# Half-row modulation units on TensorE beside the input products of the feed-forward blocks, and a later split of Strassen weight sums

## The chip, the cores and the metric

One NeuronCore of a Trainium2 chip runs the whole kernel in one launch; the other cores have nothing to do. The metric is device time in microseconds (us) from start to end of the program. The engines are named as in the profile: PE (TensorE; PEld is its weight load, which runs beside it), DVE (VectorE), ACT (ScalarE), POOL (GpSimd) and SP (SyncE, whose queue SPq issues nearly all DMAs here).

## The reference

Two layers; each is a feed-forward block (FFN), a mixer (retention and grouped attention in layer 0, neighbourhood attention in layer 1), and a second FFN, on 512 latent and 128 context tokens of width 1024. Each of the six sub-layers s takes three vectors (shift, scale, gate) from a modulation, a product of a conditioning vector with a 1024 x 9216 matrix per layer; latent and context tokens have a conditioning vector each.

```python
def swiglu(h, w_in, w_out):
    gate, up = jnp.split(h @ w_in, 2, axis=-1)
    return (jax.nn.silu(gate) * up) @ w_out            # D_FF = 2816

def adaln_sublayer(x, mod, s, g_pre, g_post, fn, weight):
    shift, scale, gate = mod[:, 3 * s, None], mod[:, 3 * s + 1, None], mod[:, 3 * s + 2, None]
    h = rmsnorm(x, g_pre) * (1 + scale) + shift
    y, aux = fn(h)
    return x + weight * gate * rmsnorm(y, g_post), aux

mod = (jax.nn.silu(cond) @ mod_w[l] + mod_b[l]).reshape(cond.shape[0], 9, 1024)
```

Everything is float32. A row of the modulation in what follows is one of the nine 1024-wide vectors of a layer, (layer, row); a half row is 512 columns of it, for both conditioning vectors.

## The kernel before

**Blocks and parts.** The four FFNs are called F1 to F4 in the order they run: layer 0 first and second, layer 1 first and second. Function `ffn` (L575 on) cuts the 22 column tiles of D_FF into six parts p0 to p5 of 2, 4, 4, 4, 4, 4 tiles (`PARTS`). A part has an input stage (activations times `w_in`, then SiLU and product, into tiles `g`) and an output stage (`g` times `w_out`, added into `yacc`). Parts p1 to p5 compute the input stage by Strassen's scheme: a `Unit` (L631) is one column tile, with seven products of twelve 128x320 matmuls (`product`, L645; one matmul is L647). `strassen` (L712) runs the products of four units interleaved, 28 places in all; after each place come `stream.pump()` and `tick()`. The place called fill runs the first output products. Then `products` (L741) runs the rest of the 120 output matmuls of 128x512 (L736), with a pump and a tick between groups.

Float32 precision comes from splitting each operand in a high and a low half and adding three products of halves. `split` (L349, L350) does so for activations: ACT copies (`g`, `b` tiles), DVE subtracts. In a unit ACT copies the intermediate sum out of PSUM (L677) before the next product may add to it, and DVE adds, multiplies and splits (L671 to L703).

**Weights.** `Stream` (L60) loads raw weights by DMAs on SP (L96) into three buffers, splits them on ACT (L156, `whi`) and DVE (L157, `wlo`) into five buffers, and for each unit has POOL form sums and differences of quarters (`_combine`, L142). One of these sums, S (the tile is called `G` or `macc` in the profile), is split by ACT and DVE too. The condition is in `_room`: the split of S comes no sooner than `PARTS_LAG` = 2 pumps after POOL's instructions were issued. An engine runs its queue in order, so what is queued behind the split on ACT waits with it.

**The modulation.** The start computes the first rows on PE (L894, with `cc32`, the conditioning vectors in columns 0 and 1 of a 32-column tile). The other 16 rows, 32 half rows, are made by the generator `mod_gen` (L359) during F1 (14 half rows), F2 (6) and F3 (12); F4 has none. A half row takes eight loads of 128 x 512 (256 KB, L369, two buffers), and per load two DVE operations, one for each conditioning vector: a TENSOR_SCALAR first (L382), then SCALAR_TENSOR_TENSOR (L384) into `macc`. The sum over the 128 partitions is four matmuls with ones (L406: two column halves for two conditioning vectors, each into its own 32-column group of PE), a DVE add of the bias (L410; bias loads at L396), and four small DMAs to DRAM (L415). `tick` asks the generator for steps at a rate that weighs a place of the output stage three times as much as one of the input stage (`OUT_SHARE` = 3).

**What sets the order.** The program is written place by place as above; a scheduler then sets the order of instructions within each engine's queue, so what is written behind a place can stand some instructions earlier or later. Buffers of a pool tag are reused in turn: a load waits until the buffer's last readers are done, and holds up SP's queue meanwhile.

## Time and profile before

| | us |
|---|---|
| time, median of 3 runs (lowest, highest) | 2821.89 (2818.86, 2822.24) |
| the profiled execution | 2815.01 |
| its span in the trace | 2813.1 |
| PE busy | 2557.8 (91%) |
| PE weight loads | 2257.3 (80%) |
| DVE busy | 2051.6 (73%) |
| ACT busy | 1176.1 (42%) |
| POOL busy | 723.6 (26%) |
| DMA, mean | 106 GB/s |
| chain that ended last: PE, DVE, DMA, POOL, issue, ACT | 33, 15, 6, 5, 4, 4% |

Shares of busy time are means over all stages of the program. PE's busy time counts matmuls with their pipeline, so that a gap between matmuls shows only where nothing is in flight. What a change in one stage is worth is read from that stage: the table of stretches gives the busy time of every engine between two times (one per group of parts in what follows), the timeline gives single pieces with the idle time before them in brackets and what ended it, and the list of waits adds such idle times up over the span. The lines that follow are of the code of before, numbered as in the listing above.

### The profile page before, as it was taken

The page shows a single profiled execution, that of the slowest core. Times are in us where ns is not written, and L with a number is a line of the kernel's source. Part 1 is how long each engine was busy: PE and PEld are TensorE (multiplying, and loading weights), DVE is VectorE, ACT ScalarE, POOL GpSimd, SP SyncE. Part 2 cuts the span into 40 slices and gives each one's busy share as a digit, 9 for nine tenths or more (in the row PEclk, how much of TensorE's full clock was granted, in tenths as well). Part 3 has the DMA queues.
Part 4 walks back from the last instruction along what each step waited for, and adds up shares of the span by engine and source line. Part 5 has one row for each costly group of instructions (what it writes and reads, how often), then busy time and mean ns, then how long its engine had stood idle before and what let it go on. Part 6 is the DMA issues. An engine that isn't in the chain of part 4 may idle for free.

```text
span 2813.1 us, 39476 instructions
## 1 busy us (share of the span) xinstructions
PE 2557.8 (91%) x15090; PEld 2257.3 (80%) x15090; DVE 2051.6 (73%) x3079; ACT 1176.1 (42%) x2179; POOL 723.6 (26%) x612
## 2 busy tenths in 40 slices
PE   7889876999999989999988998999899999999998
PEld 5778766888876788888877887788889978888887
DVE  5988886775577597787568988896777766655556
ACT  4423322364356443333354332233565555433333
POOL 1312322220001132323233222222532312323222
PEclk9999988999999999999999999999999999999999
DMA  8354564331110333343343444454222232222233
GB/s 237 105 150 133 153 174 125 106 117 55 56 49 16 94 116 108 107 129 82 98 135 116 130 145 119 130 151 123 86 67 65 65 100 75 83 80 62 77 105 112
DMA packets 358620, 297.85 MB, mean 106 GB/s; under 512 B 46352, under 2 KB 290976, under 8 KB 358432
## 3 DMA queue, kind: packets, MB, share of 16 engines
q1 hardware_dynamic: 353968, 282.24, 34.4%
q10 hardware_dynamic: 2880, 9.18, 0.8%
q0 software_dynamic: 1584, 3.93, 0.5%
q8 instruction: 118, 1.93, 0.3%
q14 instruction: 70, 0.57, 0.1%
HBM read 283.22 MB, written 15.97 MB: 106 GB/s over the span
## 4 chain that ended last, share of the span: by engine, by line
PE 33%; DVE 15%; DMA 6%; POOL 5%; issue 4%; ACT 4%; SPq 0%; DVEq 0%; ACTq 0%; POOLq 0%
PE ps L647 12%; PE ps L736 10%; DVE wlo L157 5%; PE ps L560 5%; DVE macc L384 4%; DMA mraw<-in_mod_w_dram 3%; POOL raw L142 2%; ACT whi L156 2%; PE ps L978 2%; POOL G L142 1%; DMA raw<-in_ffn_w_in_dram 1%; PE ps L550 1%; DMA raw<-in_ffn_w_out_dram 1%; DVE g L350 1%; PE ps L1925 1%
## 5 line engine op out<-in xcount | busy, mean ns | idle before, releaser
L156 ACT CAST whi<-raw 128x1024 fp32r<-128x1024 f32 x400 | 418.6, 1050 | 503.4 <-PE ps L736 239.4
L736 PE MATMUL ps<-whi,g 128*128 128x512 f32 x1760 | 586.6, 408 | 39.5 <-DVE g L350 19.8
L647 PE MATMUL ps<-hT,whi 128*128 128x320 f32 x2560 | 576.2, 313 | 2.0 <-DVE xn L688 1.9
L157 DVE TENSOR_TENSOR wlo<-raw,whi 128x1024 fp32r<-128x1024 f32 x400 | 500.1, 1253 | 103.8 <-ACT whi L156 95.7
L647 PE MATMUL ps<-b,whi 128*128 128x320 f32 x1920 | 448.2, 320 | 112.3 <-ACT xn L677 56.7
L142 POOL TENSOR_TENSOR raw<-raw 128x512 f32<-128x512 f32 x160 | 223.4, 1396 | 1256.9 <-DVE wlo L157 1191.1
L384 DVE SCALAR_TENSOR_TENSOR macc<-mraw,cc,macc 128x512 f32<-128x512 f32 x448 | 402.7, 931 | 71.7 <-DMA mraw<-in_mod_w_dram 70.9
L736 PEld LDWEIGHTS ps<-whi,g 128*128 128x128 f32 x1760 | 341.7, 195 | 135.0 <-DVE g L350 25.4
L647 PEld LDWEIGHTS ps<-hT,whi 128*128 128x128 f32 x2560 | 436.9, 192 | 8.0 <-DVE xn L688 2.6
L647 PEld LDWEIGHTS ps<-b,whi 128*128 128x128 f32 x1920 | 330.1, 194 | 134.7 <-ACT xn L677 65.7
L647 PE MATMUL ps<-hT,wlo 128*128 128x320 f32 x1280 | 399.6, 312 | 0.0
L736 PE MATMUL ps<-wlo,g 128*128 128x512 f32 x880 | 355.9, 404 | 0.0
L647 PE MATMUL ps<-b,wlo 128*128 128x320 f32 x960 | 303.6, 316 | 22.4 <-DVE wlo L157 22.4
L560 PE MATMUL ps<-hT,whi 128*128 128x384 f32 (+1 forms) x1216 | 277.6, 316 | 0.1
L647 PEld LDWEIGHTS ps<-hT,wlo 128*128 128x128 f32 x1280 | 244.6, 191 | 0.4 <-issue 0.4
L560 PEld LDWEIGHTS ps<-hT,whi 128*128 128x128 f32 x1216 | 203.9, 188 | 21.9 <-issue 15.2
L647 PEld LDWEIGHTS ps<-b,wlo 128*128 128x128 f32 x960 | 186.8, 195 | 22.8 <-DVE wlo L157 22.8
L736 PEld LDWEIGHTS ps<-wlo,g 128*128 128x128 f32 x880 | 171.7, 195 | 37.7 <-issue 0.4
L560 PE MATMUL ps<-hT,wlo 128*128 128x384 f32 (+1 forms) x608 | 188.6, 310 | 0.0
L156 ACT CAST whi<-G 128x512 fp32r<-128x512 f32 x72 | 44.6, 620 | 254.1 <-POOL G L142 118.7
L550 PE MATMUL ps<-hT,whi 128*128 128x384 f32 (+1 forms) x640 | 140.9, 311 | 4.8 <-DVE hT L350 4.8
L157 DVE TENSOR_TENSOR wlo<-G,whi 128x512 fp32r<-128x512 f32 x72 | 84.4, 1173 | 71.8 <-ACT whi L156 71.1
(402 smaller groups left out, 3846.2 us busy)
## 6 DMA issues: line engine op xcount, KB each, us to landing
raw<-in_ffn_w_in_dram SPq DMA_DIRECT2D x172, 512.0 KB
mraw<-in_mod_w_dram SPq DMA_DIRECT2D x256, 256.0 KB
raw<-in_ffn_w_out_dram SPq DMA_DIRECT2D x88, 512.0 KB
raw<-in_na_w_qkv_dram SPq DMA_DIRECT2D x24, 512.0 KB
raw<-in_ab_w_in_dram SPq DMA_DIRECT2D x22, 512.0 KB
raw<-in_mod_w_dram SPq DMA_DIRECT2D x32, 256.0 KB
xs<-x ACTq DMA_DIRECT2D x15, 512.0 KB
b<-xs SPq DMA_DIRECT2D x15, 512.0 KB
```

The source lines that it names most:

```text
L142: self.nc.gpsimd.tensor_tensor(out=out, in0=in0, in1=in1, op=op)
L156: self.nc.scalar.copy(hi[:, :k * n], raw[:, :k * n])
L157: self.nc.vector.tensor_tensor(out=lo[:, :k * n], in0=raw[:, :k * n], in1=hi[:, :k * n].bitcast(F32), op=ALU.subtract)
L350: return a, nc.vector.tensor_tensor(out=lo, in0=src, in1=hi.bitcast(F32), op=ALU.subtract)
L384: nc.vector.scalar_tensor_tensor(out=acc[c], in0=raw, scalar=w, in1=acc[c], op0=ALU.mult, op1=ALU.add)
L550: nc.tensor.matmul(out=banks[grp], lhsT=w[a][:, k, :], rhs=hT[b][:, k, o:o + n], start=(k == 0 and (a, b) == (0, 0)), stop=(k == NK - 1 an ...
L560: nc.tensor.matmul(out=banks[grp], lhsT=w[a][:, k, :], rhs=hT[b][:, k, o:o + n], start=(k == 0 and (a, b) == (0, 0)), stop=(k == NK - 1 an ...
L647: nc.tensor.matmul(out=out, lhsT=w[a][:, k, :], rhs=b[c][:, k, :], start=start and (k, a, c) == (0, 0, 0), stop=(k == 3 and (a, c) == PASS ...
L736: nc.tensor.matmul(out=out, lhsT=g[a][kf][:, t * 128:(t + 1) * 128], rhs=w[b], start=(kf == 0 and (a, b) == (0, 0)), stop=(kf == len(fts) ...
L978: nc.tensor.matmul(out=y[t][h], lhsT=hT[a][:, k, t * 128:(t + 1) * 128], rhs=ws[k // 2, h][b][:, k % 2, :], start=(k == 0 and (a, b) == (0 ...
L1925: nc.tensor.matmul(out=acc[r, c], lhsT=v, rhs=PT[hh][:, slot, c], start=(slot == 0), stop=(slot == 3))
```

## The change

The list `MOD_ROWS` deals the 16 rows to the blocks anew: F1 12 half rows (before 14), F2 8 (6), F3 10 (12), F4 2 (0). A class `Modulation` takes the place of `mod_gen`. It has units of two kinds. A "v" unit is the old way on DVE: one is written beside the output stage of each of p0 to p4 (in F4 of p0 and p1), 17 in all; its sum by ones falls to the next part's start. A "t" unit is on PE: the 32-column conditioning tile `cc32` is the stationary operand and the raw weights, 128 columns to each of four column groups of PE, the moving one; it has two steps of sixteen 32x128 matmuls (four row blocks of 128 times four column groups), each on two loads. They are written beside the input stage: two units in each of p1 to p3 and one in p4 of F1, one in p1 to p3 of F2, two in p1 and one in p2 to p4 of F3, none in F4: 15 in all. Loads are now of two row blocks (512 KB) in three buffers, a tag (`mod`) that the accumulator, the sums S of the last part and a scratch tile share; bias and result rows have one buffer (`mrow`) for two before. `PARTS_LAG` goes from 2 to 4: the split of S may come two pumps later. No tick follows the first `glu` calls of F1 any more.

```diff
-PARTS_LAG = 2
+PARTS_LAG = 4
...
+MOD_ROWS = {
+    (0, 0): [(0, 2), (0, 3), (0, 4), (0, 5), (0, 6), (0, 7)], (0, 2): [(0, 8), (1, 0), (1, 1), (1, 2)],
+    (1, 0): [(1, 3), (1, 4), (1, 5), (1, 6), (1, 7)], (1, 2): [(1, 8)],
+}
...
-OUT_SHARE = 3
...
-    def mod_gen(pool, todo):
...
+    class Modulation:
+        N = 512
+        STEPS = {"v": NK + 3, "t": 4}
+        def __init__(self, pool, todo):
+            self.pool = pool
+            self.units = [(l, r, h) for l, r in todo for h in range(D // self.N)]
+            self.loads = [(*u, q) for u in self.units for q in range(NK // 2)]
+            self.raws = []
+            self.cc32 = pool.tile([128, NK, 32], F32, tag="cc32", name="cc32", bufs=1)
+            nc.vector.memset(self.cc32, 0.0)
+            nc.vector.tensor_copy(self.cc32[:, :, 0:2], cc)
+            self.it, self.rate, self.owed = iter(()), 0.0, 0.0
+            self.load()
+        def load(self):
+            while self.loads and len(self.raws) < 2:
+                l, r, h, q = self.loads.pop(0)
+                raw = self.pool.tile([128, 2, self.N], F32, tag="mod", name="mod", bufs=3)
+                c0 = r * D + h * self.N
+                nc.sync.dma_start(out=raw, in_=kblock(I["mod_w"][l], 2 * q, 2, c0, self.N))
+                self.raws.append(raw)
+        def bias(self, l, c0, parts):
+            n = self.N // 2 if len(parts) == 4 and parts[0][1] == parts[2][1] else self.N // 4
+            row = self.pool.tile([128, 256], F32, tag="mrow", name="mrow", bufs=1)[:, 0:n]
+            for p, o in parts:
+                nc.sync.dma_start(
+                    out=row[p:p + 32, :], in_=I["mod_b"][l, c0 + o:c0 + o + n].partition_broadcast(32)
+                )
+            return row, n
+        def on_v(self, l, r, h):
+            c0 = r * D + h * self.N
+            parts = [(64 * c + 32 * e, 256 * e) for c in range(2) for e in range(2)]
+            row, n = self.bias(l, c0, parts)
+            acc = self.pool.tile([128, 2, self.N], F32, tag="mod", name="mod", bufs=3)
+            for k in range(NK):
+                raw = self.raws[0]
+                for c in range(2):
+                    w = cc[:, k, c:c + 1]
+                    if k == 0:
+                        nc.vector.tensor_scalar(out=acc[:, c], in0=raw[:, 0], scalar1=w, scalar2=None, op0=ALU.mult)
+                    else:
+                        nc.vector.scalar_tensor_tensor(
+                            out=acc[:, c], in0=raw[:, k % 2], scalar=w, in1=acc[:, c], op0=ALU.mult, op1=ALU.add
+                        )
+                if k % 2:
+                    self.raws.pop(0)
+                    if k < NK - 1:
+                        self.load()
+                yield
+            yield
+            yield
+            ps = bank([128, n])
+            for p, o in parts:
+                nc.tensor.matmul(
+                    out=ps[p:p + 32, :], lhsT=ones[:, 0:32], rhs=acc[:, p // 64, o:o + n], start=True, stop=True
+                )
+            nc.vector.tensor_tensor(out=row, in0=ps, in1=row, op=ALU.add)
+            for p, o in parts:
+                nc.sync.dma_start(out=modrows[l][r][p // 64:p // 64 + 1, h * self.N + o:h * self.N + o + n], in_=row[p:p + 1, :])
+            self.load()
+            yield
+        def on_t(self, l, r, h):
+            c0 = r * D + h * self.N
+            parts = [(32 * e, 128 * e) for e in range(4)]
+            row, n = self.bias(l, c0, parts)
+            ps = bank([128, n])
+            for q in range(NK // 4):
+                for i in range(2):
+                    raw = self.raws.pop(0)
+                    for k2 in range(2):
+                        k = 4 * q + 2 * i + k2
+                        for p, o in parts:
+                            nc.tensor.matmul(
+                                out=ps[p:p + 32, :], lhsT=self.cc32[:, k, :], rhs=raw[:, k2, o:o + n],
+                                start=(k == 0), stop=(k == NK - 1),
+                            )
+                self.load()
+                yield
+            nc.vector.tensor_tensor(out=row, in0=ps, in1=row, op=ALU.add)
+            for p, o in parts:
+                nc.sync.dma_start(out=modrows[l][r][:, h * self.N + o:h * self.N + o + n], in_=row[p:p + 2, :])
+            yield
+        def stage(self, kind, n, places):
+            for _ in self.it:
+                pass
+            us, self.units = self.units[:n], self.units[n:]
+            self.it = itertools.chain(*((self.on_v if kind == "v" else self.on_t)(*u) for u in us))
+            self.rate, self.owed = self.STEPS[kind] * len(us) / places, 0.0
+        def tick(self):
+            self.owed += self.rate
+            while self.owed >= 1.0:
+                self.owed -= 1.0
+                next(self.it, None)
...
-        side, steps = side or (iter(()), 0)
-        weight = sum(7 * n for n in PARTS[1:-1]) + sum(4 * n for n in PARTS[:-1]) * OUT_SHARE
-        rate, owed = steps / (weight - 6.0), 0.0
+        mod = Modulation(fp, todo)
+        n_v = len(PARTS) - 1
+        n_t = [0] + [max(len(mod.units) - n_v + 3 - p, 0) // 4 for p in range(4)]
...
-        def tick(share=1):
...
+        def tick():
             if prep:
                 prep.pop(0)()
+            mod.tick()
...
             else:
-                for _ in side:
-                    pass
-                stream.part_tile = lambda: fp.tile([128, 512], F32, tag="macc", name="macc", bufs=2)
+                mod.stage("t", len(mod.units), 1)
+                mod.stage("t", 0, 1)
+                stream.part_tile = lambda: fp.tile([128, 512], F32, tag="mod", name="mod", bufs=3)
...
             else:
+                if not last:
+                    mod.stage("t", n_t[p], 7 * len(fts))
                 strassen(fts, g, fill)
...
             if not last:
-                for _ in todo:
+                mod.stage("v", 1, 4 * len(fts) - 1)
+                for _ in outs:
                     stream.pump()
-                    tick(OUT_SHARE)
+                    tick()
```

In the new code's numbering, used in the order below: L411 and L413 are the DVE operations of a v unit, L425 and L428 its sum and add, L445 and L451 matmuls and add of a t unit, L387 the loads, L395 the bias, L430 and L453 the rows out; L690 is the unit product (before L647), L779 the output product (L736), L804 the add into `yacc` (L761), L353 the low half of the activation split (L350), L159 and L160 the weight split (L156, L157), L99 the raw weight load (L96).

**PE, F1.** In before, four ones matmuls stand in the middle of the output products of p1:

```order
L736 MATMUL ps<-wlo,g_1_911 128x512
L736 MATMUL ps<-whi,g_1_915 128x512
L406 MATMUL ps<-macc,ones 32x256 x4
L736 MATMUL ps<-whi,g_2_912 128x512
L736 MATMUL ps<-wlo,g_2_912 128x512
L736 MATMUL ps<-whi,g_2_916 128x512
```

In the new code this is PE's queue about place 4 of p2's input stage, where the first step of a t unit stands:

```order
L690 MATMUL ps<-hT_97,whi 128x320
L690 MATMUL ps<-hT_98,whi 128x320
L690 MATMUL ps<-hT_97,wlo 128x320
L445 MATMUL ps<-mod,cc_722 32x128 x16
L690 MATMUL ps<-b_718,whi 128x320
L690 MATMUL ps<-b_719,whi 128x320
L690 MATMUL ps<-b_718,wlo 128x320
```

The step comes between two products of the units, and 16 matmuls are in one step; the ones matmuls of v units stand at the start of a part.

**DVE, F1, end of p2's input stage.** `g_2` and `g_3` are the activation splits of the third and fourth unit; the output products need them. Before:

```order
L384 SCALAR_TENSOR_TENSOR macc<-mraw,cc,macc 128x512
L688 TENSOR_TENSOR tok<-tok,ps 128x320
L384 SCALAR_TENSOR_TENSOR macc<-mraw,cc,macc 128x512
L693 TENSOR_TENSOR tok<-tok,ps 128x320
L384 SCALAR_TENSOR_TENSOR macc<-mraw,cc,macc 128x512
L350 TENSOR_TENSOR g_3_1757<-tok,g_3_1753 128x320
L157 TENSOR_TENSOR wlo<-raw,whi 128x1024
L701 TENSOR_TENSOR tok<-tok,ps 128x320
L157 TENSOR_TENSOR wlo<-raw,whi 128x1024
L703 TENSOR_TENSOR tok<-tok 128x320
L384 SCALAR_TENSOR_TENSOR macc<-mraw,cc,macc 128x512
L350 TENSOR_TENSOR g_3_1757<-tok,g_3_1753 128x320
```

And now:

```order
L731 TENSOR_TENSOR tok<-tok,ps 128x320
L413 SCALAR_TENSOR_TENSOR mod<-mod,cc 128x512 x5
L736 TENSOR_TENSOR tok<-tok,ps 128x320
L413 SCALAR_TENSOR_TENSOR mod<-mod,cc 128x512
L353 TENSOR_TENSOR g_3_1723<-tok,g_3_1719 128x320
L160 TENSOR_TENSOR wlo<-raw,whi 128x1024
L744 TENSOR_TENSOR tok<-tok,ps 128x320
L160 TENSOR_TENSOR wlo<-raw,whi 128x1024
L746 TENSOR_TENSOR tok<-tok 128x320
L413 SCALAR_TENSOR_TENSOR mod<-mod,cc 128x512
L353 TENSOR_TENSOR g_3_1723<-tok,g_3_1719 128x320
```

Ahead of the last `g_3` split and behind `g_2` seven operations of a v unit stand, before four; behind it, in the output stage, only the adds into `yacc` follow where before the modulation went on.

**DVE and SP, F1, p4.** `g_0` is the first unit's split; `wlo<-G` is the low half of S, which place 9 of PE needs. DVE before, up to and with that split:

```order
L384 SCALAR_TENSOR_TENSOR macc<-mraw,cc,macc 128x512
L350 TENSOR_TENSOR g_0_3447<-xn,g_0_3443 128x640
L384 SCALAR_TENSOR_TENSOR macc<-mraw,cc,macc 128x512 x6
L382 TENSOR_SCALAR macc<-mraw,cc 128x512 x2
L384 SCALAR_TENSOR_TENSOR macc<-mraw,cc,macc 128x512 x14
L157 TENSOR_TENSOR wlo<-G_3431,whi 128x512
L157 TENSOR_TENSOR wlo<-raw,whi 128x1024 x3
```

And now:

```order
L746 TENSOR_TENSOR xn<-xn 128x320
L451 TENSOR_TENSOR mrow<-ps,mrow 128x128
L353 TENSOR_TENSOR g_0_3383<-xn,g_0_3379 128x640
L411 TENSOR_SCALAR mod<-mod,cc 128x512 x2
L413 SCALAR_TENSOR_TENSOR mod<-mod,cc 128x512 x14
L160 TENSOR_TENSOR wlo<-G_3372,whi 128x512
L160 TENSOR_TENSOR wlo<-raw,whi 128x1024 x3
```

22 modulation operations became 16 between the two. On SP the loads behind them stood before as

```order
L369 DMA mraw<-in_mod_w_dram 128x512 x3
L415 DMA mod_7_106<-mrow_3416 1x256 x4
L369 DMA mraw<-in_mod_w_dram 128x512 x2
L396 DMA mrow_4088<-in_mod_b_dram 32x256 x4
L369 DMA mraw<-in_mod_w_dram 128x512 x11
L96 DMA raw<-in_ffn_w_in_dram 128x8x128 x3
```

and now as

```order
L395 DMA mrow<-in_mod_b_dram 32x128 x4
L477 DMA mcol<-mod_6_105 128x8x1
L387 DMA mod<-in_mod_w_dram 128x2x512 x3
L453 DMA mod_7_106<-mrow 2x128 x4
L387 DMA mod<-in_mod_w_dram 128x2x512
L395 DMA mrow<-in_mod_b_dram 32x256 x4
L387 DMA mod<-in_mod_w_dram 128x2x512
L99 DMA raw<-in_ffn_w_in_dram 128x8x128 x3
```

Of the three loads in one row the first is the last of the t unit, the other two are the v unit's first; its third and fourth stand behind the t unit's rows out and the v unit's bias.

## Rows read from the trace of the kernel before

**Rows 1.** Table of stretches: F1 p1-p3, F1 p4, F2, F3, F4 p1-p4.

```profile
core 0: us, PE busy (x) PEld busy (x) DVE busy (x) ACT busy (x) POOL busy (x), PEclk, DMA share, GB/s
93.50:393.00 299.50, 261.80 (x1450) 228.86 (x1449) 266.15 (x338) 92.82 (x139) 87.77 (x74) 0.93 0.52 149
393.00:512.40 119.40, 84.76 (x490) 74.92 (x489) 90.11 (x121) 29.97 (x45) 23.22 (x16) 0.86 0.47 125
1034.60:1380.40 345.80, 324.36 (x1873) 294.91 (x1872) 253.22 (x310) 122.28 (x183) 93.86 (x64) 0.98 0.37 107
1530.20:1912.30 382.10, 341.76 (x1921) 302.10 (x1920) 336.02 (x418) 121.52 (x183) 99.22 (x64) 0.95 0.46 133
2396.00:2723.50 327.50, 311.63 (x1826) 287.33 (x1825) 184.00 (x221) 121.87 (x183) 88.64 (x64) 1.00 0.27 79
```

**Rows 2.** Timeline of PE: start, us, engine, line, operation; in brackets idle before.

```profile
368.63 0.79 PE L736 MATMUL ps<-whi,g 128*128 128x512 f32 x1 [4.51 <-DVE g L350]
...
1748.82 0.90 PE L647 MATMUL ps<-b,whi 128*128 128x320 f32 x2 [5.45 <-ACT tok L677]
...
1796.31 1.22 PE L736 MATMUL ps<-whi,g 128*128 128x512 f32 x2 [1.93 <-DVE g L350]
```

**Rows 3.** Timeline of ACT, F2 p2.

```profile
1129.31 0.62 ACT L156 CAST whi<-G 128x512 fp32r<-128x512 f32 x1 [3.94 <-POOL G L142]
```

**Rows 4.** List of waits: us in total, times, longest.

```profile
ACT whi L156 <- POOL G L142: 118.7, 46, 5.2
...
PE ps L647 <- ACT xn L677: 56.7, 33, 3.3
```

**Rows 5.** Timeline of PE, F1 p4.

```profile
418.33 0.90 PE L647 MATMUL ps<-b,whi 128*128 128x320 f32 x2 [8.60 <-ACT whi L156]
...
441.67 0.64 PE L647 MATMUL ps<-b,wlo 128*128 128x320 f32 x1 [22.43 <-DVE wlo L157]
```

**Rows 6.** Timeline of DVE, F1 p4.

```profile
427.09 1.42 DVE L384 SCALAR_TENSOR_TENSOR macc<-mraw,cc,macc 128x512 f32<-128x512 f32 x2 [1.40 <-DMA mraw<-in_mod_w_dram]
...
440.93 0.68 DVE L157 TENSOR_TENSOR wlo<-G,whi 128x512 fp32r<-128x512 f32 x1
```

**Rows 7.** Timeline of SP's queue, F1 p4.

```profile
420.04 21.33 SPq L369 DMA_DIRECT2D mraw<-in_mod_w_dram  x11
```

**Rows 8.** Costliest groups (page, part 5): count, busy us, mean ns, idle before.

```profile
L384 DVE SCALAR_TENSOR_TENSOR macc<-mraw,cc,macc 128x512 f32<-128x512 f32 x448 | 402.7, 931 | 71.7 <-DMA mraw<-in_mod_w_dram 70.9
```

**Rows 9.** Timeline of PE about a set of ones products, F1 p2.

```profile
244.42 0.31 PE L647 MATMUL ps<-hT,wlo 128*128 128x320 f32 x1
...
244.86 0.31 PE L647 MATMUL ps<-hT,wlo 128*128 128x320 f32 x1
245.10 0.64 PE L406 MATMUL ps<-macc,ones 128*32 128x256 f32 x8
...
246.06 0.31 PE L647 MATMUL ps<-b,wlo 128*128 128x320 f32 x1
```

**Rows 10.** Timeline of PE about a conditioning product, start of the program.

```profile
47.71 1.07 PE L894 MATMUL ps<-raw,cc 128*32 128x256 f32 x16
48.71 0.62 PE L937 MATMUL ps<-hT,whi 128*128 128x384 f32 x2
```

**Rows 11.** One line's weight loads (L894): ns min, median, max; first and last start.

```profile
L894 PEld LDWEIGHTS ps<-raw,cc x128: 106/110/178, 20.5 to 58.1; 128*32 128x32 f32 x128
```

**Rows 12.** Chain that ended last, pieces in order: start us, us, what.

```profile
983.06 6.30 DMA mraw<-in_mod_w_dram
...
1217.71 2.77 DMA mraw<-in_mod_w_dram
1222.41 3.96 DMA mraw<-in_mod_w_dram
1237.71 4.27 DMA mraw<-in_mod_w_dram
```

**Rows 13.** Timeline of PE, F4 p0, first output product.

```profile
2382.89 0.80 PE L736 MATMUL ps<-whi,g 128*128 128x512 f32 x1 [5.58 <-ACT g L349]
```

More of the change, by code (lines that the diff above doesn't have):

```diff
@@ L570, in pair_banks, with ffn @@
         return [(bank([128, 384]), b[:, u, :]) for u in range(2)]
[L573 removed]
+    def ffn(fp, l, s, pending, todo, nxt, banks0=None):
         j = s // 2
@@ L2043, in hybrid_flow_kernel @@
     pending = None
-    rows_of = lambda l, s: [(l, 3 * s + r) for r in range(3)]
     for i, (l, s) in enumerate(subs):
@@ L2051, in hybrid_flow_kernel @@
         else:
-            todo = [] if i else [(l, 3 * s + 2)]
-            for n in range(i + 1, len(subs)):
-                todo += rows_of(*subs[n])
-                if subs[n][1] != 1:
-                    break
             banks0 = None
```

67 lines of the change are left out of this document (4 added, 63 removed).

## The prediction

> **What bounds the kernel now.** I read the table of stretches first. TensorE (PE) is the busiest engine in all of them, so the four feed-forward blocks (F1 to F4 in the order they run) decide, and their parts p1 to p4 are alike: 28 places of twelve 128x320 products (336 in all), then 120 output products. F4 has no modulation, and its four parts take 327.5 us [rows 1], 81.8 us each, at a granted clock of 1.00: that is the floor of a part. The twelve parts of F1 to F3 take 299.5 + 119.4 + 345.8 + 382.1 = 1146.8 us [rows 1] against 12 x 81.8 = 981.6. **165.2 us lie above the floor, where the modulation runs.** VectorE (DVE) is busy for 266 of 299.5 us in F1 and 336 of 382 in F3, and for 184 of 327.5 in F4.
>
> The excess is no single wait. At the start of output products PE waits for the split of the last activation tile, 4.51 and 1.93 us; at a unit's second product it waits for a copy on ScalarE, 5.45 us in F3 [rows 2]. That copy (L677) is late in two ways. ScalarE stands 3.94 us for GpSimd's weight sum before it splits it [rows 3], a wait with 46 instances and 118.7 us over the span, and PE waits 56.7 us for one of the two tiles that L677 writes, `xn` [rows 4]. In F1's p4 PE loses 8.60 us and then 22.43 us in one piece [rows 5]: DVE must do 22 modulation operations, each pair behind a load, before it splits the weights that place 9 needs [rows 6], and SyncE stands 21.33 us on these loads [rows 7], since each needs a buffer that DVE frees.
>
> **The change part by part.** *VectorE.* 15 of 32 half rows leave it, each with 14 operations of 931 ns [rows 8] and two first ones: 15 x 14 x 0.931 = 196 us less busy time. By itself this pays nothing; it pays where PE waits on DVE, or on what stands behind DVE.
>
> *The ones products.* The sum over partitions of a DVE unit takes four products. From 244.42 to 244.86 three ordinary products start; from 244.86 to 246.06 three more and the four ones products [rows 9], so one such set costs 1.20 - 0.44 = 0.76 us. 32 sets become 17, now one at the start of a part: 0.8 us each.
>
> *Modulation on TensorE.* 15 units of two steps, 30 steps. No row shows such a step. Nearest is the conditioning product before the first block: 8 products of 32 columns by 256, four column groups side by side, 1.00 us to the next product [rows 10]. A step has twice the products at half the width, the same columns in all: 1.0 us, and 0.2 for entry and exit, taken from the ones products: 1.2 us. The lower end is 1.0; the upper is 2.0, if a 128-wide product costs what a 256-wide one does. A part with two units pays 4.8 us, with one 2.4. In all PE gains 30 x 1.2 = 36 us of work and loses 15 x 0.76 = 11.
>
> The order puts the steps before places 4, 8, 15 and 18 where a part has two units, before 8 and 15 where it has one. A step eats two loads of 512 KB; of the next two the first can be under way, the second waits for this step's buffer. Loads take 2.77 to 6.30 us in the chain [rows 12]; the steps stand 5 to 12 us apart, so most are hidden. In F1's p4 they stand before 8 and 9, one place apart (12 x 0.44 / 3 = 1.8 us [rows 9]), and there it is paid.
>
> *VectorE's units.* They are written beside the output products but the order runs them earlier, ahead of the last activation split. So PE can wait at the start of output products as before. I take 4.5 us with two units in the part (the row of 4.51), and 1.9 us for the other waits; with one unit 1.9 in all (the row of 1.93) [rows 2]. Bounds: 0 to 10, and 0 to 4. In F4's p0 DVE gets eight operations ahead of such a split, 8 x 0.931 = 7.4 us; PE already waits 5.58 us there for ScalarE [rows 13], so part is covered; I take 5.5, bounds 0 to 12.
>
> *F1's p4.* Sixteen DVE operations instead of 22 stand ahead of the weight split, behind four loads of which the last two wait for buffers that DVE itself frees. Counted from the second step's end: the unit's second load lands after 4.2 us (between 3.96 and 4.27 [rows 12]), its four operations take 2 x 1.42 = 2.8 [rows 6], the fourth load is issued then, lands after 4.2, and four more take 2.8: 14 us, and 0.6 for the split. Before it, the second step waits 4.2 - 1.8 = 2.4 us for its load. PE's clock falls to its half level (1.2 GHz) while it idles and stays there for a while: a mean of 0.86 over 119.4 us [rows 1] is 0.14 / 0.5 x 119.4 = 33.4 us at half, 2.4 more than the two waits (8.60 and 22.43); I add 2.4. Together 19.4. Bounds 5 (the loads early) to 33 (as before).
>
> *S split two pumps later* (PARTS_LAG 2 to 4). It moves ScalarE's wait for GpSimd behind the copies that PE waits for. In F4 the sums cost PE nothing, so GpSimd alone is not late; I expect most of the waits on L677 to go, and this is inside the 1.9 us. The split sum is used several places after its split, so a later one costs nothing; if that cover were gone, it would be one place, 1.8 us, per sum. The loads move the same bytes as before, in half as many issues: 0; what they could cost is rival C. Which wait is late next where L677's is gone? The activation splits, which are in the sum.
>
> **Sum.** F1 p1 to p3: 3 x (81.8 + 0.8 + 4.8 + 4.5 + 1.9) = 281.4, before 299.5: -18.1. F1 p4: 81.8 + 0.8 + 2.4 + 1.9 + 19.4 = 106.3, before 119.4: -13.1. F2: 3 x 86.9 + 84.5 (no step in p4) = 345.2, before 345.8: -0.6. F3: 93.8 + 3 x 86.9 = 354.5, before 382.1: -27.6. That is -59.4. Against it: F4 two sets of ones products and the wait at p0, 1.5 + 5.5 = 7.0; the last parts of F1 to F3 one set each, 2.3. **Net -50 us** (-50.1). The profiled execution took 2815.0 us, span 2813.1 and 1.9 around it; 2765 by it. The median of the runs is 6.9 us above, so 2772.
>
> **Rivals.** *A: the steps and nothing else.* If every wait that DVE caused goes, two-unit parts cost 89.3, F1 p4 90 and F4 only its 1.5: 4 x 4.5 + 16.3 + 5.5 = 40 us more, -90, 2732. For it: PE has no gap in F4, where DVE has 44% of the time to itself. Against: the order still has DVE operations ahead of activation splits. Chance 0.14.
>
> *B: the waits change place only.* The activation split is 10 us late in two-unit parts and 4 us in one-unit parts: 4 x 5.5 + 6 x 2.1 = 35 us back, -15, 2807. The order speaks for it, the 196 us off DVE against it. Chance 0.14.
>
> *C: slower, by loads.* Before, only DVE waited for modulation loads; now PE does, with everything behind it. If each of the 30 steps waits 4 us for its second load (3.96 in the chain [rows 12]), that is 120 - 50 = +70, 2892; the side turns at 50 / 30 = 1.7 us a step. For it: SyncE stood 21.33 us on such issues in F1's p4 [rows 7], and weight loads are queued behind them. Against: steps lie further apart than a load takes, and all bytes together keep the DMA engines busy for 0.52 of F1's time at most [rows 1]. Chance 0.09; a third of it lands within 0.2%.
>
> *D: weight loads do not hide.* In the conditioning product 16 weight loads of 110 ns each lie within the 1.00 us, four at a time, the next four beside running products [rows 10, 11]. If they did not overlap, a step would take eight times 0.11 us more, 30 x 0.88 = 26 us: 2798. Chance 0.05. The Trainium skill, "TensorE: Matmul & The Clock Gate", "Part 3: Packing small matmuls", says that weight loads overlap running products only where the row group differs; a step's column groups all use the same rows. By that rule this rival would be the case; the trace's row speaks against it.
>
> **How the numbers follow.** Forecast 0.56, A 0.14, B 0.14, C 0.09, D 0.05, and 0.02 that the order ties something together that I don't see. The forecast's own spread, from a step of 1.0 to 1.6 us and half of each bound, is 2752 to 2793. The range runs from A to a little above B: 2730 to 2816. About 0.2% (5.6 us) is what can be told from no change: B's upper tail and part of C lie there. Faster 0.84, same 0.06, slower 0.10.
>
> **What would show it.** A step of 1.0 to 1.3 us and mostly no wait for the mod loads ahead of it (C and the upper bound fall otherwise). Waits of PE on the L677 copies near nothing in F2 and F3. One-unit parts of 86 to 88 us, two-unit parts of 92 to 96, F1's p4 of 100 to 110 with a wait behind place 9. At F4's p0 a longer wait ahead of output products. It is wrong if PE waits for loads before most steps, if the splits ahead of output products are over 8 us late, or if weight loads for the input products arrive late because SyncE stands on modulation loads.

## The result and the profile after

The changed kernel took 2788.8 us (median of 4 runs, 2786.0 to 2796.7) against 2822.1 for the kernel before: a ratio of 0.988, with an interval of 0.986 to 0.991. That is 33 us faster, where 50 was forecast and the range reached from -92 to -6. Its profiled execution spans 2784.2 us, 28.9 less than the one before.

The table of stretches of the changed kernel, for the same parts as [rows 1] (F1 p1 to p3, F1 p4, F2, F3 and F4 p1 to p4), and then F3's p2 and p3 alone:

```profile
core 0: us, PE busy (x) PEld busy (x) DVE busy (x) ACT busy (x) POOL busy (x), PEclk, DMA share, GB/s
99.80:387.90 288.10, 259.71 (x1782) 231.63 (x1781) 178.57 (x230) 90.71 (x136) 81.75 (x74) 0.96 0.50 148
387.90:487.90 100.00, 82.89 (x531) 75.09 (x528) 55.55 (x75) 29.98 (x46) 21.61 (x16) 0.93 0.37 108
1012.40:1366.90 354.50, 330.57 (x2053) 301.33 (x2049) 235.86 (x296) 122.66 (x183) 91.09 (x64) 0.97 0.39 114
1519.80:1877.80 358.00, 334.23 (x2180) 303.17 (x2176) 233.89 (x299) 122.88 (x183) 89.95 (x64) 0.98 0.42 126
2363.90:2695.10 331.20, 315.87 (x1837) 290.79 (x1834) 197.32 (x240) 121.67 (x182) 90.71 (x64) 0.99 0.28 82
1613.60:1700.30 86.70, 81.16 (x533) 73.62 (x529) 57.60 (x76) 30.31 (x46) 22.16 (x16) 1.00 0.42 124
1700.30:1791.20 90.90, 85.36 (x533) 77.85 (x529) 57.64 (x74) 30.37 (x46) 22.17 (x16) 0.94 0.39 119
```

DVE is no longer near full anywhere (179 of 288 us in F1, before 266 of 300), and still each part of F1 to F3 lies 4.0 to 18.3 us above the floor of 81.8. By stretch:

| | before | forecast | after |
|---|---|---|---|
| F1 p1 to p3 | 299.5 | 281.4 | 288.1 |
| F1 p4 | 119.4 | 106.3 | 100.0 |
| F2 p1 to p4 | 345.8 | 345.2 | 354.5 |
| F3 p1 to p4 | 382.1 | 354.5 | 358.0 |
| F4 p1 to p4 | 327.5 | 329.0 | 331.2 |

From before to after these add up to -42.5 us. The rest of the program is 13.6 us longer, where 7.8 was forecast; 6.4 of the 13.6 is one wait at the start of F1's p1.

The list of waits of the changed kernel (us, times, longest) shows that PE waits for ScalarE's copies (now L720) for 89.7 us, as before (90.2), and that ScalarE's wait for GpSimd's S has grown from 118.7 [rows 4] to 152.5:

```profile
ACT whi L159 <- POOL G L145: 152.5, 52, 4.3
...
PE ps L690 <- ACT xn L720: 51.0, 28, 2.9
...
PE ps L690 <- ACT tok L720: 38.7, 18, 2.6
```

**What a step costs.** PE's timeline about a step of F2's p2:

```profile
1135.74 0.31 PE L690 MATMUL ps<-hT,wlo 128*128 128x320 f32 x1
1135.98 1.08 PE L445 MATMUL ps<-mod,cc 128*32 128x128 f32 x32
1136.99 0.56 PE L690 MATMUL ps<-hT,whi 128*128 128x320 f32 x2
1137.38 0.31 PE L690 MATMUL ps<-hT,wlo 128*128 128x320 f32 x1
```

The step's 16 matmuls are 32 records. It is 1.01 us from its start to the next product, and 0.2 in all before and behind it: the 1.2 us of the forecast. The profile of that line adds who it waited for: 2.4 us in 3 cases for loads, of 30 steps. So rival C is out as far as the steps' own waits go. D is out too: the step's 32 weight loads lie inside its 1.01 us.

```profile
1135.98 0.81 PEld L445 LDWEIGHTS ps<-mod,cc 128*32 128x32 f32 x32 [0.19 <-issue]
...
L445 PEld LDWEIGHTS ps<-mod,cc x960: 105/110/111, 109.4 to 1822.9; 128*32 128x32 f32 x192
...
  DMA mod<-in_mod_w_dram: 2.4, 3
```

The Trainium skill, "TensorE: Matmul & The Clock Gate", "Part 3: Packing small matmuls", has weight loads overlap running products only across row groups; here loads of column groups overlapped, and the measurement decides.

**Where PE waits.** In one-unit parts there are two waits for L720, with ScalarE's queue ahead of the first:

```profile
1127.55 0.90 PE L690 MATMUL ps<-b,whi 128*128 128x320 f32 x2 [2.62 <-ACT tok L720]
...
1145.69 0.56 PE L690 MATMUL ps<-b,whi 128*128 128x320 f32 x2 [2.87 <-ACT xn L720]
```
```profile
1123.17 0.62 ACT L159 CAST whi<-G 128x512 fp32r<-128x512 f32 x1 [3.59 <-POOL G L145]
1123.70 0.47 ACT L745 ACTIVATE xn<-xn 128x320 f32<-128x320 f32 x1
1124.43 1.05 ACT L159 CAST whi<-raw 128x1024 fp32r<-128x1024 f32 x1 [0.27 <-POOL raw L145]
1126.45 0.72 ACT L352 CAST g<-xn 128x640 fp32r<-128x640 f32 x1 [0.98 <-DVE xn L746]
1127.08 0.42 ACT L720 COPY tok<-ps 128x320 f32<-128x320 f32 x1
```

ScalarE stands 3.59 us for S. Behind it stand the SiLU (L745) of the previous unit, its product on DVE, its split (L352), and last the copy for which PE waits. This wait is not only there where modulation runs. F4's p2 in the kernel before, which has none, shows it at places 4, 11 and 18:

```profile
2486.32 0.56 PE L647 MATMUL ps<-b,whi 128*128 128x320 f32 x2 [0.82 <-ACT xn L677]
...
2500.41 0.56 PE L647 MATMUL ps<-b,whi 128*128 128x320 f32 x2 [1.51 <-ACT tok L677]
...
2514.48 0.56 PE L647 MATMUL ps<-b,whi 128*128 128x320 f32 x2 [1.51 <-ACT xn L677]
```

Counted from one start on PE to the next, as in what follows, each is 0.2 us longer than its bracket: 1.0, 1.7 and 1.7 us. They are inside the floor of 81.8. In the changed kernel a one-unit part has them at places 11 and 18 (F2's p1 at 4 as well), but 2.8 and 3.0 us long.

Two more pieces are F1's p4, where the 16 operations on DVE shown in the order (L411, L413) still hold up the weight split, and the start of F1's p1, where PE waits for p0's unit on DVE, since the ones products now stand there:

```profile
420.70 0.63 PE L690 MATMUL ps<-b,wlo 128*128 128x320 f32 x1 [12.11 <-DVE wlo L160]
...
98.75 0.64 PE L425 MATMUL ps<-mod,ones 128*32 128x256 f32 x2 [6.38 <-DVE mod L413]
```

### The profile page after: what moved, and what is told of

Its sections match the earlier page's. It is cut to its first block, busy times and chain, and to the rows that moved or that the text cites. A ratio compares the mean times of both kernels' runs of the same rounds, so it can differ in the third digit from the quotient of the medians.

```text
span 2784.2 us, 40608 instructions
## 1 busy us (share of the span) xinstructions
PE 2563.5 (92%) x15930; PEld 2275.5 (82%) x15930; DVE 1845.4 (66%) x2847; ACT 1178.1 (42%) x2179; POOL 703.3 (25%) x612
## 4 chain that ended last, share of the span: by engine, by line
PE 42%; DVE 11%; POOL 6%; ACT 4%; issue 3%; DMA 2%; DVEq 0%; ACTq 0%; POOLq 0%; SPq 0%
PE ps L690 15%; PE ps L779 13%; PE ps L607 5%; DVE wlo L160 3%; PE ps L1023 3%; POOL raw L145 3%; PE ps L597 2%; ACT whi L159 2%; POOL G L145 2%; DVE mod L413 1%; PE ps L1970 1%; DVE mod L411 1%; ACT g L352 1%; DMA mod<-in_mod_w_dram 1%; PE ps L1951 1%
## 5 line engine op out<-in xcount | busy, mean ns | idle before, releaser
L159 ACT CAST whi<-raw 128x1024 fp32r<-128x1024 f32 x400 | 418.7, 1050 | 475.9 <-PE ps L779 225.1
L779 PE MATMUL ps<-whi,g 128*128 128x512 f32 x1760 | 574.6, 403 | 40.3 <-ACT g L352 26.6
L160 DVE TENSOR_TENSOR wlo<-raw,whi 128x1024 fp32r<-128x1024 f32 x400 | 495.8, 1242 | 140.2 <-ACT whi L159 129.9
L690 PE MATMUL ps<-hT,whi 128*128 128x320 f32 x2560 | 577.1, 313 | 0.0
L145 POOL TENSOR_TENSOR raw<-raw 128x512 f32<-128x512 f32 x160 | 216.7, 1354 | 1241.2 <-DVE wlo L160 1138.3
L690 PE MATMUL ps<-b,whi 128*128 128x320 f32 x1920 | 444.4, 319 | 93.0 <-ACT xn L720 51.0
L690 PEld LDWEIGHTS ps<-hT,whi 128*128 128x128 f32 x2560 | 433.1, 191 | 12.9 <-DVE x L804 5.3
L779 PEld LDWEIGHTS ps<-whi,g 128*128 128x128 f32 x1760 | 339.7, 193 | 122.6 <-ACT g L352 29.4
L690 PEld LDWEIGHTS ps<-b,whi 128*128 128x128 f32 x1920 | 329.7, 194 | 110.4 <-ACT xn L720 61.3
L690 PE MATMUL ps<-hT,wlo 128*128 128x320 f32 x1280 | 399.6, 312 | 0.0
L779 PE MATMUL ps<-wlo,g 128*128 128x512 f32 x880 | 353.7, 402 | 0.0
L690 PE MATMUL ps<-b,wlo 128*128 128x320 f32 x960 | 303.6, 316 | 12.1 <-DVE wlo L160 12.1
L607 PE MATMUL ps<-hT,whi 128*128 128x384 f32 (+1 forms) x1216 | 277.9, 317 | 0.0
L690 PEld LDWEIGHTS ps<-hT,wlo 128*128 128x128 f32 x1280 | 244.4, 191 | 0.0
L413 DVE SCALAR_TENSOR_TENSOR mod<-mod,cc 128x512 f32<-128x512 f32 x238 | 201.0, 880 | 17.7 <-DMA mod<-in_mod_w_dram 17.7
L779 PEld LDWEIGHTS ps<-wlo,g 128*128 128x128 f32 x880 | 170.0, 193 | 37.4
L690 PEld LDWEIGHTS ps<-b,wlo 128*128 128x128 f32 x960 | 186.2, 194 | 12.4 <-DVE wlo L160 12.4
L804 DVE TENSOR_TENSOR x<-x,ps 128x512 f32<-128x512 f32 x160 | 107.6, 685 | 92.2 <-PE ps L779 91.5
L159 ACT CAST whi<-G 128x512 fp32r<-128x512 f32 x72 | 44.7, 621 | 263.5 <-POOL G L145 152.5
L160 DVE TENSOR_TENSOR wlo<-G,whi 128x512 fp32r<-128x512 f32 x72 | 73.0, 1014 | 118.3 <-ACT whi L159 118.1
```

The costliest lines, as they stand in the source:

```text
L145: self.nc.gpsimd.tensor_tensor(out=out, in0=in0, in1=in1, op=op)
L159: self.nc.scalar.copy(hi[:, :k * n], raw[:, :k * n])
L160: self.nc.vector.tensor_tensor(out=lo[:, :k * n], in0=raw[:, :k * n], in1=hi[:, :k * n].bitcast(F32), op=ALU.subtract)
L413: nc.vector.scalar_tensor_tensor(out=acc[:, c], in0=raw[:, k % 2], scalar=w, in1=acc[:, c], op0=ALU.mult, op1=ALU.add)
L607: nc.tensor.matmul(out=banks[grp], lhsT=w[a][:, k, :], rhs=hT[b][:, k, o:o + n], start=(k == 0 and (a, b) == (0, 0)), stop=(k == NK - 1 an ...
L690: nc.tensor.matmul(out=out, lhsT=w[a][:, k, :], rhs=b[c][:, k, :], start=start and (k, a, c) == (0, 0, 0), stop=(k == 3 and (a, c) == PASS ...
```

## The experiments

Ratios are against the kernel before in the same session (its median 2815.7 to 2816.8); times are medians. The changed kernel's 2788.8 us was measured beside 2822.1 for the kernel before. So a difference from it in us is some 5 us larger than its ratio gives: 18 us are 12 by the ratios, 78 are 73. No reading below turns on that.

### The lag alone, on the kernel before

```diff
-PARTS_LAG = 2
+PARTS_LAG = 4
```

> The kernel before with PARTS_LAG 4 instead of 2 and nothing else. Theory of the prediction (the lag moves the split of S behind the copies that PE waits for): the waits of PE on these copies, 90.2 us in the kernel before (56.7 for xn, 33.5 for tok), fall by a third or more, and the time by 10 to 25 us, to 2797 to 2812. Rival (the scheduler sets ScalarE's order by data and not by the place where the split is written; the order of this kernel differs from before in 12 rows of ScalarE): the waits stay at 80 to 95 us and the time within 6 us of 2822.

2816.1 us, ratio 1.000 (0.9995 to 1.0012). The waits on the two copies are 53.9 and 40.6 us. The rival holds for the kernel before: the lag sets only the place at which the split is written, and the scheduler decides where it stands on ScalarE. No run takes the lag of the changed kernel back to 2, so for that kernel it is not shown.

### S without its dependence on the split

```diff
-            (G[:, a], G[:, a], U[:, a], ALU.subtract), (S, U[:, b], G[:, a], ALU.subtract),
-            (U[:, a], U[:, a], U[:, b], ALU.add), (G[:, b], G[:, b], S, ALU.subtract),
+            (S, G[:, a], U[:, a], ALU.subtract), (S, U[:, b], S, ALU.subtract), (U[:, a], U[:, a], U[:, b], ALU.add),
+            (G[:, a], U[:, b], S, ALU.subtract), (G[:, b], G[:, b], S, ALU.subtract),
```

> The changed kernel, with GpSimd's weight sums in another order: S is formed from the raw quarters without overwriting them, so it no longer waits until VectorE has split those quarters; this takes five GpSimd operations per unit instead of four (80 more of some 1.35 us, 108 us). Theory S (PE's remaining waits for ScalarE's copies, 51.0 and 38.7 us, come from the split of S standing in ScalarE's queue until GpSimd, itself released by VectorE's split, has S ready): ScalarE's wait for S (152.5 us) falls under 40, PE's waits for the copies under 40, also in F4 and the last parts that have no modulation, and the time falls by 40 to 80 us against the changed kernel, to 2710 to 2750. Rival (VectorE's modulation operations between the unit's own are the cause): the waits fall by less than a quarter, the time stays at 2780 to 2800 or rises by what GpSimd's extra work takes.

2792.4 us, ratio 0.991 (0.989 to 0.993): the same as the changed kernel. Theory S failed. ScalarE's wait for S fell from 152.5 to 17.4 us, but PE's waits for the copies only from 89.7 to 74.2. In one-unit parts those at place 11 fell (2.6 us in brackets, now 0.9 to 1.9), those at 18 hardly did. So S being late is not the whole of it: the split of the previous unit still stands ahead of the copy. And the edit has a price. GpSimd's operations, 80 more, now run beside DVE's weight splits instead of behind them (its wait for such splits fell from 1138 to 40 us); its busy time went from 703 to 873 us, and those splits from 1242 to 1392 ns each, 60 us over 400. Even F4's p2, without modulation, grew from 81.1 to 85.0. The Trainium skill, "SBUF — State Buffer", "SBUF: two separate sides", says that a VectorE operation with two SBUF inputs and a GpSimd operation that reads SBUF lock each other out; these splits are of that kind, and the trace agrees.

### GpSimd's bias transfers one part later

```diff
-            if p == 3 and first:
+            if p == 4 and first:
                 spread_bias(g[0][0])
```

> The changed kernel with the 27 GpSimd transfers of the relative bias issued in F1's p4 instead of its p3. Theory (the scheduler runs the sixteen VectorE operations ahead of the split of S in p4 because GpSimd's sum stands behind those transfers there): PE's wait of 12.11 us in F1's p4 is gone, and part of the 4.68 us at the start of p3's output products; 10 to 16 us less than the changed kernel, 2773 to 2779. Rival (the operations stand there because their loads make them ready): a wait of 8 us or more stays in p4 and the time within 6 us of 2789. A third possibility is that the same wait of some 12 us turns up in p5.

2788.9 us, ratio 0.990 (0.988 to 0.991). The wait of 12.1 us in p4 is gone, as the theory has it, and F1's p1 to p4 take 376 us for 388; the second step of p4 moved as well, from before place 9 to before 15. But the time did not fall. Part of the wait came back in p5 (2.9 us at place 9, 2.9 at place 13), and the stretch from p5 to F2's p1 grew by 5.2 us. F3 lost 8.5 us, most of it in parts whose waits are the same as in the changed kernel. Its p2:

```profile
1607.80:1698.70 90.90, 85.35 (x532) 77.87 (x528) 57.68 (x76) 30.06 (x46) 22.16 (x16) 0.94 0.40 119
```

The same part took 86.7 us at a granted clock of 1.00 in the changed kernel, and p3 there 90.9 at 0.94 (rows above), with waits of 2.8 and 3.0 us in all three. Behind such a wait the clock is sometimes at its half level (1.2 GHz) and sometimes not.

### The ones products later

```diff
+            if places == 1 or kind == "v":
+                for _ in self.it:
+                    pass
...
+            if kind == "v":
+                self.rate, self.owed = (self.STEPS[kind] - 1) * len(us) / places, 0.0
+            else:
+                self.it = itertools.chain(self.it, *gens)
+                self.rate, self.owed = (self.STEPS[kind] * len(us) + 1) / places if us else 0.25, 0.0
```

> The changed kernel with the ones products of a VectorE unit written some four places into the next part instead of at its start. Theory (PE stands 6.38 us at the start of F1's p1 because the unit of p0 is not ready, and a unit that ends later keeps fewer of its operations ahead of activation splits): that wait falls under 2 us and the time by 5 to 12 us against the changed kernel, 2777 to 2784. Rival (the accumulator holds its buffer some 5 us longer, so that the loads of the next TensorE unit come late): the steps on TensorE wait 1 to 2 us each for loads instead of 2.4 us in all, in 17 parts, 10 to 25 us slower, 2799 to 2814.

2728.5 us, ratio 0.969 (0.968 to 0.971): 60 us less than the changed kernel, five times the most that was expected, and not for the reason given. A wait of 7.8 us for a DVE unit stayed. Two other things had moved with the ones products. In eight of the twelve parts p1 to p4 of F1 to F3, 7 of a unit's 16 operations now stood behind the last activation split. And the steps on PE stood elsewhere, at places 17 and 23 in most one-unit parts for 8 and 15; at place 18 PE no longer waits there. The next runs separate the two.

### DVE's operations forced behind the split

```diff
+            ccv = self.pool.tile([128, NK, 2], F32, tag="ccv", name="ccv", bufs=1)
+            nc.vector.scalar_tensor_tensor(
+                out=ccv.rearrange("p k c -> p (k c)"), in0=self.after, scalar=0.0,
+                in1=cc.rearrange("p k c -> p (k c)"), op0=ALU.mult, op1=ALU.add,
+            )
...
-                    w = cc[:, k, c:c + 1]
+                    w = ccv[:, k, c:c + 1]
...
+                mod.after = g[1][len(fts) - 1][:, TOK - 2 * NK:TOK].bitcast(F32)
                 mod.stage("v", 1, 4 * len(fts) - 1)
```

> The changed kernel, with each VectorE unit's factors copied by one small VectorE operation that reads the last activation split of the input stage, so that all its 16 operations stand behind that split in VectorE's queue (in the changed kernel the order has all 16 ahead of it in p1 to p4); the ones products stay at the start of the next part. Theory Q (what is left of PE's waits comes from these operations standing ahead of activation splits and of the units' own operations): PE's waits at the start of output products and part of those for ScalarE's copies go, 30 to 60 us less than the changed kernel, 2730 to 2760. Rival P (it was the place of the ones products that counted in the run that moved them): the time stays at 2780 to 2800, and PE waits 1 to 4 us for the ones products at the start of most parts, since the units end later.

2771.1 us, ratio 0.984 (0.983 to 0.985): 18 us less. PE's waits for DVE's activation splits, 13.6 us in the changed kernel, are down to 1.6; but it now waits 30.3 us at the start of the four p1 for p0's unit, and 85.6 us for the copies. One-unit parts take 89 to 91 us, with 2.8 us at places 11 and 18 as before. So theory Q explains F1, whose p1 to p3 take 17.4 us less, and not F2 (4.3 less) and F3 (0.1 more).

> The same forced order, and the ones products four places into the next part. In the run that only moved the ones products 7 of 16 operations had come behind the last split in most parts. Theory Q: 0 to 15 us less than that run (2728), since nothing stands ahead of the splits any more. Rival P (only the place of the ones products counts): the same as that run within 5 us. A third possibility is that 16 operations beside the output products hold up the additions of these and the weight splits, 10 us or more slower than that run.

2736.8 us, ratio 0.972 (0.971 to 0.973): 34 us less than without the later ones products, though every operation was behind the split in both. 8 us more than the run that only moved the ones products. The operations ahead of the splits were not what that run had gained. What was left is the place of the ones products themselves and the places of the steps; the runs with shifted steps separate these.

### Leaving out one kind of unit

The first run leaves out the 17 DVE units (loads, operations, sums), the second the 15 units on PE; their rows hold the bias alone.

> The changed kernel without the loads, operations, ones products and adds of the 17 VectorE units; their rows hold the bias alone. It gives what these units cost in their place. Theory Q: 55 to 85 us less than the changed kernel, 2704 to 2734, and PE's waits for ScalarE's copies per part at the level of F4's parts without modulation. Rival R (the remaining waits come from GpSimd, ScalarE and the steps on TensorE): only the 13 us of ones products and the 6.4 us wait at F1's p1 go, 2765 to 2775.

2736.7 us, ratio 0.973 (0.971 to 0.974). 52 us less, short of what theory Q asked and more than rival R allowed. But in F2 and F3 the waits of 2.8 us at places 11 and 18 are there without any DVE unit, and PE waits 95.2 us for the copies. F1's p4 keeps a wait of 9.2 us for the weight split, behind another DVE operation, which waits 7.4 us for a DMA of a finished row (`mcol`).

> The changed kernel without the loads, products and adds of the 15 TensorE units; their rows hold the bias alone. By the trace a step costs 1.2 us of PE's time and waits for loads come to 2.4 us in all: 38 us less than the changed kernel if the steps cost nothing beyond that, 2745 to 2757. Rival C of the prediction (the loads hold up SyncE and other waits): 55 us or more less. If the steps partly fill time in which PE would wait anyway, 15 to 30 us less.

2719.0 us, ratio 0.965 (0.964 to 0.966): 70 us less. The steps cost nearly twice their 38 us. That is above the 55 us at which rival C was to hold, but this run takes away the loads and the steps together; the changed kernel with its steps three places later (below) keeps every load and every step and is 8 us faster still, so the loads aren't the cause. The other half is what the steps do to others. PE's waits for activation splits on DVE fell from 13.6 to 3.4 us, the wait of 12.1 us in F1's p4 is 0.4, and the mean granted clock rose from 0.971 to 0.979. The waits for the copies hardly fell in total (89.7 to 87.8).

### The steps three places later

```diff
-            self.rate, self.owed = self.STEPS[kind] * len(us) / places, 0.0
+            self.rate = self.STEPS[kind] * len(us) / places
+            self.owed = -3 * self.rate if kind == "t" else 0.0
```

> The run with VectorE's unit operations forced behind the last activation split, and one change to it: the steps on TensorE stand three places later, before places 11 and 18 in parts with one unit (before: 8 and 15) and before 7, 11, 18 and 21 in parts with two. Theory M (a step three places ahead of a place where PE waits for ScalarE's copy turns the order on ScalarE: the split of S, which waits for GpSimd, stands ahead of the unit's SiLU, 38 times in the order of the changed kernel and 18 in this one): the waits at 11 and 18, 2.8 us each in the one-unit parts of F2 and F3, fall to 1.7 or less, these parts from 89.3 to 82 to 86 us, and the time by 20 to 40 us, from 2771 to 2731 to 2751. Rival (the step itself lengthens every wait behind it, wherever it stands): one-unit parts stay at 88 to 90 us and the time within 6 us of 2771.

2713.5 us, ratio 0.964 (0.962 to 0.965): 58 us less than the forced run, from the places of the steps alone, where 20 to 40 were expected. Five of the six one-unit parts take 81.7 us, as F4's parts do without modulation, and F2 and F3 run at a granted clock of 1.00 (F2, F3, and F2's p2 alone; then F2's p2 of the forced run):

```profile
979.80:1309.50 329.70, 321.10 (x2050) 293.10 (x2048) 235.40 (x298) 120.88 (x181) 90.73 (x64) 1.00 0.43 124
1467.80:1800.40 332.60, 325.93 (x2179) 296.38 (x2177) 237.92 (x301) 120.70 (x181) 90.81 (x64) 1.00 0.47 136
1063.60:1145.30 81.70, 80.65 (x533) 73.54 (x529) 58.44 (x75) 30.07 (x46) 22.43 (x16) 1.00 0.47 132
...
1085.00:1174.40 89.40, 84.09 (x532) 76.59 (x528) 58.06 (x75) 30.34 (x46) 22.10 (x16) 0.96 0.41 121
```

Place 11 of F2's p2, on PE and on ScalarE:

```profile
1083.21 0.31 PE L696 MATMUL ps<-hT,wlo 128*128 128x320 f32 x1
1083.45 1.08 PE L450 MATMUL ps<-mod,cc 128*32 128x128 f32 x32
1085.02 0.56 PE L696 MATMUL ps<-b,whi 128*128 128x320 f32 x2 [0.49 <-ACT tok L726]
```
```profile
1080.93 0.47 ACT L751 ACTIVATE xn<-xn 128x320 f32<-128x320 f32 x1 [1.26 <-DVE xn L750]
1083.40 0.62 ACT L159 CAST whi<-G 128x512 fp32r<-128x512 f32 x1 [2.00 <-POOL G L145]
1083.93 0.72 ACT L352 CAST g<-xn 128x640 fp32r<-128x640 f32 x1
1084.56 0.42 ACT L726 COPY tok<-ps 128x320 f32<-128x320 f32 x1
1084.87 1.05 ACT L159 CAST whi<-raw 128x1024 fp32r<-128x1024 f32 x1
```

Two things differ from the rows of the changed kernel. The step fills PE's wait: 0.49 us are left of it. And ScalarE's order is another: the SiLU (L751) runs ahead of S, its split and the copy follow S at once, and the split of the raw weights comes behind the copy. With the steps at 8 and 15 the SiLU's input comes 1.2 us later, and the scheduler puts S, with its wait for GpSimd, first. In the trace of the changed kernel the split of S stands directly ahead of that SiLU 20 times: just before places 11 and 18, in each of the ten parts with steps at 8 and 15. It does so 20 times in the forced run and in the run without DVE units too, and 22 times where the bias transfers came later and F1's p4 also had its steps at 8 and 15. It never does in the kernel before, in the run without steps, or in any run whose steps stand elsewhere. (The run that forms S in another way is left out of this count.)

> The changed kernel with the same shift of the steps by three places and nothing else (the loads of the VectorE units come later by it, so that 7 of their 16 operations fall behind the last split in half of the parts). Theory M with the operations ahead of splits as a second cause: 25 to 55 us less than the changed kernel, 2734 to 2764, with the largest part in F2 and F3. Rival (F1's waits for activation splits and its 12 us wait in p4 are all that the later run gained): F2 and F3 keep their lengths and the time falls by less than 15 us.

2711.1 us, ratio 0.9625 (0.961 to 0.964): 78 us less than the changed kernel and more than was expected, from this one edit. F2's p1 to p4 ran at a granted clock of 0.99 (0.97):

```profile
970.00:1309.00 339.00, 326.08 (x2053) 295.24 (x2049) 230.42 (x296) 121.65 (x183) 91.32 (x64) 0.99 0.41 120
```

F1 p1 to p3 took 260.1 us (288.1), p4 88.2 (100.0), F2 339.0 (354.5), F3 342.1 (358.0); PE's waits for the copies fell to

```profile
PE ps L691 <- ACT xn L721: 33.1, 28, 2.6
...
PE ps L691 <- ACT tok L721: 23.8, 30, 2.3
```

In two-unit parts the steps stand before 7, 11, 18 and 21, and PE's waits at 11 and 18 are 0.5 us there too. With the later steps the loads of DVE's units come later, and 7 of 16 operations fall behind the last split by themselves in the four two-unit parts, 3 in two others. In F2 none do, and its 15.5 us are the steps' places alone. F1's p4 lost its 12.1 us wait although the bias transfers stand where they stood. This run does all the work and is 26 us faster than the one that left the DVE units out.

Part of the 78 us is the clock: its mean over the program rose from 0.971 to 0.985. In the rows of F3's p2 and p3 above 0.06 less of the clock over 91 us cost 4.2 us; by that, as an estimate, 0.014 over 2784 us are some 30 of the 78.

### Everything together

> A version put together from the findings: VectorE's operations behind the last activation split; ones products some four places into the next part, in p0 too; the steps on TensorE at the places that follow from it (17 and 23 in most one-unit parts); the bias transfers on GpSimd in F1's p4. If the causes add up: against the forced run with late ones products (2737) the 29 us that PE waits at the start of four p1 for the unit of p0 fall to under 10, 2712 to 2722. If DVE can't finish the unit of p0 in time wherever the ones products stand: 2730 to 2740.

2713.4 us, ratio 0.9635 (0.962 to 0.965). At the lower end of what was expected, and no better than the shift alone. The 29 us that PE waited for the units of p0 are gone, but it now waits 15.5 us in the four p1 for another of ScalarE's copies.

> The same without forcing VectorE's operations behind the split (7 of 16 fall behind it by themselves in most parts). Against the run that only moved the ones products (2728): the 7.8 us wait at the start of F1's p1 and part of F1's p4 go, 2714 to 2724. If forcing is worth more than the small operation that it needs, the other version is 3 to 10 us faster than this one; if not, they are within 3 us.

2741.2 us, ratio 0.973 (0.971 to 0.974): a miss, 13 us worse than the run that only moved the ones products, where 4 to 14 less were expected. With the bias transfers in p4 the wait for a weight split moved on to F1's p5:

```profile
478.89 0.55 PE L696 MATMUL ps<-b,whi 128*128 128x320 f32 x2 [2.88 <-ACT whi L159]
```

The stretch from F1's p5 to F2's p1 took 533.0 us for 523.5, and F1's p1 97.3 for 91.1; the cause of the latter is open.

## Why the prediction was right, and what it missed

*The direction and the range* held. The run without steps shows the two sides of the sum: it is 98 us faster than the kernel before, where the forecast without its steps comes to 88, and the steps took back 64 to 70 us, where 38 had been reckoned. So the relief of DVE was sized about right, and what the steps cost at their places was not.

*The step's price* itself (1.2 us), *the ones products* as work and *the loads* were right, and with them rivals C and D fell.

*F1's p4* was forecast at 106.3 us and took 100.0. The place and the cause were right, the term too large: DVE waited once for a load, 1.48 us, where two waits of more than 4 us had been reckoned, since the unit's first loads were there when it began.

*The one-unit parts* are the term that failed. They were forecast at 86.9 and took 86.6 to 91.1. The step behind it reads "It moves ScalarE's wait for GpSimd behind the copies that PE waits for. In F4 the sums cost PE nothing, so GpSimd alone is not late; I expect most of the waits on L677 to go". The waits on these copies stayed at 89.7 us (90.2), and the prediction's own sign, that they would be near nothing in F2 and F3, was not met. The lag moves nothing in the kernel before (ratio 1.000). F4 was misread, and rival A repeats it ("PE has no gap in F4"): its parts have three such waits each, 4.4 us, so most of them are not an excess at all. And the added steps, at 8 and 15, made the two that stayed longer, 2.8 to 3.0 us for 1.7. Where the clock stayed at 1.00 a one-unit part took 86.6 to 86.7, close to the forecast, but by luck: the 1.9 us above the floor were taken from a late activation split, and the 1.7 us that came are waits for the copies, which the prediction took to go. The others, at 0.94 to 0.98, took 88.1 to 91.1; the sum has a clock term in F1's p4 alone. F2 shows it best: forecast unchanged, measured 8.7 us longer.

*The two-unit parts* were forecast at 93.8 and took 93.2 to 98.4. The wait for the last activation split, taken at 4.5 us in each from the longest row of before, was that long only in F1's p3; in the other three it was 1.9. Waits for ScalarE's part of these splits (in F1), longer waits for the copies and a clock of 0.95 to 0.98 stood in its place, so that 93.2 and 93.8 came out by luck.

*What the sum left out* was a wait for the ones products themselves: 6.4 us at the start of F1's p1. They had been priced as 0.8 us of work; placed at the head of a part, they also wait for a unit that isn't done. *F4's p0* was forecast 5.5 us longer; its wait grew by 1.9:

```profile
2351.43 0.80 PE L779 MATMUL ps<-whi,g 128*128 128x512 f32 x1 [7.50 <-ACT g L352]
```

Taken together: the gain fell short by 17 us, and the two runs that only moved the steps show that their places, not their amount, cost more than that. That ScalarE's turned order is what lengthens the waits rests on the rows and the counts; no run set that order by itself, and the run that brought S early shortened only the first of the two waits.

## What to carry to other kernels

Work that is added to the busiest engine costs by its place: in one-unit parts, at a place where the engine waits anyway, these steps cost nothing; three places earlier all 30 of them cost nearly twice their length. A stretch that is taken as a floor may hold regular waits, so list its waits before pricing what will go. Where a scheduler sets the order, an edit of the place at which something is written is to be read in the new order of every engine, also of those that the edit doesn't name.

## What the runs showed of the hardware

Parts with the same work and the same waits of 2.8 and 3.0 us took 86.7 or 90.9 us, at a granted clock of 1.00 or 0.94; F4's undisturbed parts, with waits of 1.7 us and less, were granted 1.00. Four column groups of 32 on PE ran a step's 32 recorded products and their 32 weight loads in 1.01 us, so most of the loads ran beside products. When GpSimd's sums, 80 more of them, ran beside 400 weight splits on DVE instead of behind them, these took 0.15 us longer each.
